# Merge of a two-layer mixer trunk: latent heads' products first, and a planner with twelve more, randomly shifted plans

## The chip, the cores and the metric

One core of one Trainium2 chip runs the whole program. The metric is device time in microseconds (us) of one execution; the kernel before was run three times for it, and once more under the profiler.

## The reference

Two layers over x of 512 positions by 1024 channels, float32. In each layer

```
h = rmsnorm(x); p = h @ w_in            # columns: three mixers, their gates, three merge gates
o_a = latent attention (8 heads, low-rank q and kv, rotary part) * silu(gate_a)
o_b = forgetting attention (8 heads, cumulative log forget gate) * silu(gate_b)
o_c = RWKV-7 time mixing (8 heads, delta-rule state) * silu(gate_c)
merged = sigmoid(g_a) * (o_a @ w_pa) + sigmoid(g_b) * (o_b @ w_pb) + sigmoid(g_c) * (o_c @ w_pc)
x = x + merged @ w_out
```

o_a, o_b and o_c have 512 channels each, the merge gates g_a, g_b, g_c 1024 each. What follows is about the order in which the three products of `merged` are made.

## The kernel before, in words

Activations lie transposed: channels on 128 partitions, the 512 positions along a row. A float32 matrix product is made of two rounded parts of each operand (`split`, line 679: a high part, and what is left of it), so one product over 128 input channels is three matmuls of 128x512 (`mm3`, lines 794 to 796). Weights come from DRAM by SP's queue (`wload`, line 758) and are split on ACT, DVE or POOL (`wpart`: the high part by `copy`, line 662, the low part by `combine`, line 674).

The body of a layer is written as five generators, run by `weave`: "p" prepares the four head pairs of RWKV, "c" runs their chains (`rwkv_chain`), "y" is the attention (four pairs of latent heads, then four pairs of forgetting heads, each softmax tile going PE, DVE, ACT, DVE, PE), "z" (`merge_gates`) projects the 24 merge gates and writes tanh of each to DRAM (`thd`), and "m" (`merge`) is the merge.

`merge` waits for the four chains and the four latent pairs. It makes tiles for the split o_a (`oa`, in the buffers "At" of the chains), o_c (`oc`, in "T3" and "KR") and o_b (`ob`), and loads o_a and o_c from DRAM (`odr`; `load`, line 1541) pair by pair, through tiles of the pool "tx", which has eight buffers. Then, for each of eight blocks d of 128 output channels, it loads the gates a and c (lines 1563 and 1564, into "tx"), makes the A product of the block (12 matmuls, PSUM tag "xk"), the C product (12 matmuls, tag "ch"), and on DVE (th + 1) * product for each (line 1556, which empties the PSUM buffer); A and C are added on POOL, and kept in `sums_` for d from 3 (tiles `sum` in buffers that RWKV has left) or written to `thd` for d of 0 to 2. The B products (tags "wk", "av", "xk", "ch") follow when the forgetting heads are closed, and last the products with w_out in tag "acc". PSUM buffers: "acc" 3, "wk" 2, "xk", "ch" and "av" 1 each.

What order the instructions take on each engine is set by `plan`. It lists the program's instructions with a cost each (`_cost`) and a table of latencies between engines, and runs a list scheduler over them (`forward`): on each engine the ready instruction with the greatest urgency goes next, and some may go to ACT, DVE or POOL. Tiles of a pool tag are granted in the order of the program, and the first uses of two tiles of one tag keep that order (`ops[uses[y][0]].after.setdefault(uses[x][0], False)`). One plan is made from urgencies by longest path, then ROUNDS = 3 more from urgencies that `backward` reads off the best plan so far. Each is replayed with latencies stretched by SLACK, and the shortest replay is kept. `kernel` does so for two margins and builds the program with the better one; each engine takes its instructions in exactly that order.

Of the kernel before, what the change touches and what calls it, by code (L numbers as in the profile page):

```python
# [83 lines left out]
WIRE, AHEAD = 250, 1500  # L84
ROUNDS = 3
PB = {"acc": 3, "wk": 2, "xk": 1, "ch": 1, "av": 1}
DRY = {"raw": 4, "w": 6, "acc": 1}
# [112 lines left out]
def port(op, e, psum):  # L200

    srcs = [a for a in op.ins if a[5] > 1 or a[2] - a[1] == 1]
    if e == POOL:
        return 2 if op.kind != "InstMemset" else 1
    if e != DVE or op.kind in ("InstMemset", "InstTensorReduce", "InstStreamTranspose", "InstReciprocal"):
        return 0
    n = op.outs[0][5]
    full = [a for a in op.ins if a[0] not in psum and a[5] >= n]
    if len(full) > 1:
        return 1  # L210
    return 2 if (op.kind in ("InstTensorCopy", "InstActivation", "InstTensorScalarPtr") and len([a for a in op.ins if a[5] >= n]) == 1
                 and full and op.outs[0][0] not in psum) else 0


def plan(insts, tags, manual, flex, margin, replay=None):
# [306 lines left out]
    best = None  # L522
    for i in range(1 + ROUNDS):
        if i:
            backward(best[1][2])
        last = forward()
        stretch[0] = SLACK
        real = forward(last[0])
        stretch[0] = margin
        if best is None or max(real[2]) < max(best[0][2]):  # L530
            best = real, last
# [18 lines left out]
def build(tc, x_t, wpk, wsm, wv, vec, cst, out, order_of=None, pick={}, queues=None, margin=2.0):  # L550
# [189 lines left out]
    for l in range(L):  # L740
# [415 lines left out]

        ready, built, done, closed, zdone = [], [0], [0], [0], [0]

# [353 lines left out]
        def merge_gates():  # L1512

            for d in range(8):
                for i in range(3):
                    th = T(tag="zth", bufs=1)
                    yield from proj(f"m{'abc'[i]}{d}", "z", lambda ps: act.activation(th, ps, AF.Tanh, scale=0.5))
                    nc.sync.dma_start(thd[d, i], th)
                zdone[0] += 1
# [11 lines left out]
        def merge():  # L1531
# [18 lines left out]
            def product(w, c, o, tag, th):  # L1550
                ps = PS(tag)
                for k in range(4):
                    mm3(ps, *w(c + 128 * k, c + 128 * k + 128), *o[k], k == 0, k == 3)
                    if k % 2:
                        yield
                dve.scalar_tensor_tensor(th, th, 1.0, ps, op0=ALU.add, op1=ALU.mult)

            sums_ = [None] * 3 + kept()
            for d in range(8):
                while zdone[0] <= d:  # L1560
                    yield "wait"
                ta, tc_ = TX(), TX()
                nc.sync.dma_start(ta, thd[d, 0])
                nc.sync.dma_start(tc_, thd[d, 2])
                yield from product(wgroup(f"pab{d}", "m"), 0, oa, "xk", ta)
                yield from product(wgroup(f"pc{d}", "m"), 0, oc, "ch", tc_)
                if sums_[d] is None:
                    combine(ta, ta, tc_, ALU.add, POOL)
                    nc.sync.dma_start(thd[d, 0], ta)
                else:  # L1570
                    combine(sums_[d], ta, tc_, ALU.add, POOL)
                yield
# [20 lines left out]

        steps, ob, mgk = [], [], []
        weave([("p", rwkv_preps()), ("c", rwkv_chains()), ("y", attention()), ("z", merge_gates()), ("m", merge())],
# [24 lines left out]
    if queues is None:  # L1620
        ops, queues, start, end, picked = plan(insts, tags, manual, flex, margin)
        raise Traced(max(end), stream_order(all_steps, ops, start), picked, queues)
    for q in queues:
# [147 lines left out]
```

## Time and profile before

| | us |
|---|---|
| median of 3 runs | 1400.03 (1399.03 to 1400.41) |
| the profiled execution | 1399.46 |
| its span, first to last instruction | 1397.7 |
| PE busy | 1333.1 (95%) |
| DVE busy | 1078.8 (77%) |
| ACT busy | 943.4 (67%) |
| POOL busy | 362.5 (26%) |
| mean granted PE clock | 0.985 of full speed |

PE's busy time counts a matmul until its modelled end, and matmuls overlap, so a stretch in which PE is busy throughout can still do more or less work; the count of matmuls in a stretch tells. An engine's idle time matters here only where PE waits for it.

### The profile page before, as it was taken

How to read it: one execution, taken by the hardware profiler on the slowest of the kernel's cores; microseconds unless marked ns; L12 is line 12 of the kernel's file. 1: busy time of each engine (PE TensorE's matmuls, PEld its weight loads, DVE VectorE, ACT ScalarE, POOL GpSimd, SP SyncE). 2: the span in 40 equal slices, each digit the busy share in tenths (PEclk: the TensorE clock that was granted, in tenths of full speed). 3: DMA queues.
4: the chain of work that ended last, by engine and by line, in shares of the span. 5: the costliest groups of instructions: out<-in, count | busy, mean ns of one | idle time of the engine just before them, and what ended most of it. 6: DMA issues, size and time to landing. Idle time of an engine off the chain costs nothing. (4 is left out here: it accounts for less than half of the span.)

```text
span 1397.7 us, 25030 instructions
## 1 busy us (share of the span) xinstructions
PE 1333.1 (95%) x8532; PEld 1051.7 (75%) x8532; DVE 1078.8 (77%) x2488; ACT 943.4 (67%) x1900; POOL 362.5 (26%) x749
## 2 busy tenths in 40 slices
PE   7999999999999999799999999999999999996998
PEld 5877787878778867578877787877777768874787
DVE  8967968877897687567688679788889697886673
ACT  7658676766987787524566777776878686875341
POOL 1343351215411611000021443531264125210000
PEclk9999999999999999799999999999999999998999
DMA  5443332334143231465534343322233333324763
GB/s 179 135 119 108 91 113 70 106 92 107 43 128 91 91 95 57 126 211 177 180 97 153 100 123 94 104 80 73 88 87 89 90 114 95 106 77 131 216 203 98
DMA packets 114623, 158.67 MB, mean 114 GB/s; under 512 B 36544, under 2 KB 44608, under 8 KB 114496
## 3 DMA queue, kind: packets, MB, share of 16 engines
q1 hardware_dynamic: 114496, 157.08, 37.3%
q8 instruction: 67, 1.10, 0.3%
q14 instruction: 60, 0.49, 0.1%
HBM read 128.72 MB, written 28.31 MB: 112 GB/s over the span
## 5 line engine op out<-in xcount | busy, mean ns | idle before, releaser
L794 PE MATMUL acc<-hh,w 128*128 128x512 f32 x1008 | 372.0, 404 | 18.3 <-DVE hh L662 5.4
L662 ACT ACTIVATE w<-raw 128x256 fp32r<-128x256 f32 (+1 forms) x521 | 208.2, 412 | 254.7 <-PE acc L796 145.3
L795 PE MATMUL acc<-hl,w 128*128 128x512 f32 x1008 | 369.2, 402 | 0.6 <-DVE hl L674 0.5
L796 PE MATMUL acc<-hh,w 128*128 128x512 f32 x1008 | 368.5, 401 | 1.0 <-DVE w L674 1.0
L674 DVE TENSOR_TENSOR w<-raw,w 128x256 fp32r<-128x256 f32 (+1 forms) x598 | 251.2, 434 | 81.4 <-ACT w L662 75.0
L794 PEld LDWEIGHTS acc<-hh,w 128*128 128x128 f32 x1008 | 189.1, 189 | 60.6 <-DVE hh L662 5.4
L796 PEld LDWEIGHTS acc<-hh,w 128*128 128x128 f32 x1008 | 189.3, 189 | 39.6 <-DVE w L674 2.5
L795 PEld LDWEIGHTS acc<-hl,w 128*128 128x128 f32 x1008 | 189.2, 189 | 39.4 <-DVE hl L674 1.9
L674 POOL TENSOR_TENSOR w<-raw,w 128x256 fp32r<-128x256 f32 (+1 forms) x102 | 92.8, 915 | 395.3 <-ACT w L662 199.7
L1019 POOL TENSOR_TENSOR W<-W,NL 128x60 f32<-128x60 f32 (+24 forms) x248 | 89.4, 361 | 75.1 <-DMA NL<-d 56.8
L1226 PE MATMUL wk<-qk 96*128 96x512 f32 (+11 forms) x320 | 93.7, 326 | 2.0 <-DVE PP L674 1.4
L662 DVE CAST w<-raw 128x256 fp32r<-128x256 f32 (+1 forms) x179 | 53.4, 306 | 48.3 <-PE acc L796 42.2
L1021 POOL TENSOR_TENSOR W<-W 128x60 f32<-128x60 f32 (+24 forms) x248 | 85.3, 344 | 18.2
L1226 PEld LDWEIGHTS wk<-qk 96*128 96x128 f32 (+2 forms) x320 | 59.8, 191 | 18.1 <-DVE PP L674 8.2
L674 DVE TENSOR_TENSOR PP<-wk,PP 128x512 fp32r<-128x512 f32 (+3 forms) x128 | 61.4, 486 | 14.7 <-ACT PP L662 13.2
L1201 DVE CUSTOM_DVE_ANT_0 wk<-wk,cmask 128x128 f32<-128x128 f32 (+3 forms) x128 | 61.7, 499 | 5.4 <-PE wk L1200 3.3
L662 ACT ACTIVATE PP<-wk 128x512 fp32r<-128x512 f32 (+3 forms) x120 | 50.9, 432 | 7.8 <-PE av L1240 3.6
L1227 DVE TENSOR_TENSOR wk<-wk,dmask 128x128 f32<-128x128 f32 x128 | 37.0, 293 | 14.8 <-PE wk L1226 13.8
L1238 PE MATMUL av<-PP,Vh 128*128 128x512 f32 (+3 forms) x128 | 43.6, 340 | 3.3 <-DVE PP L662 2.0
L1231 ACT ACTIVATE wk<-wk 128x512 f32<-128x512 f32 (+1 forms) x64 | 26.8, 423 | 28.7 <-DVE wk L1227 28.2
L1240 PE MATMUL av<-PP,Vh 128*128 128x512 f32 (+3 forms) x128 | 43.7, 342 | 1.3 <-DVE PP L674 1.3
L1200 PE MATMUL wk<-qk 96*128 96x384 f32 (+7 forms) x128 | 41.1, 334 | 2.2 <-DVE ty L1201 1.8
(536 smaller groups left out, 2885.0 us busy)
## 6 DMA issues: line engine op xcount, KB each, us to landing
raw<-wpk SPq DMA_DIRECT2D x326, 256.0 KB, 2.7
tx<-thd SPq DMA_DIRECT2D x54, 256.0 KB, 3.4
thd<-zth SPq DMA_DIRECT2D x48, 256.0 KB, 2.1
tx<-odr SPq DMA_DIRECT2D x22, 256.0 KB, 2.9
raw<-wpk SPq DMA_DIRECT2D x32, 128.0 KB, 2.2
NL<-d SPq DMA_DIRECT2D x32, 128.0 KB, 2.8
odr<-sg SPq DMA_DIRECT2D x14, 256.0 KB, 2.3
x<-x_t SPq DMA_DIRECT2D x8, 256.0 KB, 4.0
```

The lines of the kernel that those rows point to most:

```text
L662: lambda q: act.activation(dst, src, AF.Copy) if q == ACT else dve.tensor_copy(dst, src))
L674: any_of(costs, lambda q: (dve if q == DVE else gp).tensor_tensor(dst, a, b, op=op))
L794: pe.matmul(ps, wh, xh, start=first, stop=False)
L795: pe.matmul(ps, wh, xl, start=False, stop=False)
L796: pe.matmul(ps, wl, xh, start=False, stop=last)
L1019: gp.tensor_tensor(tv, WL[:, 0:m, s:s + 1].broadcast_to([128, m, n]), NL[:, s:s + 1, s + 1:32].broadcast_to([128, m, n]), op=ALU.mult)
L1021: gp.tensor_tensor(WL[:, 0:m, s + 1:32], WL[:, 0:m, s + 1:32], tv, op=ALU.add)
L1200: pe.matmul(ps[:, 0:n], t[sr, A["sq"], 128 * i:n], t[sr, 2, 0:n], start=True, stop=True)
L1201: dve.tensor_tensor_reduce(out=ps[:, 0:n], in0=ps[:, 0:n], in1=cmask[:, 512 - n:512], scale=1.0, scalar=NEG, op0=ALU.add, op1=ALU.max, acc ...
L1226: pe.matmul(pv, t[rows, k, js], t[rows, q, q0:512], start=i == 0, stop=i == len(passes) - 1)
L1238: pe.matmul(av[:, q0:512], vh, ph, start=j == 0, stop=False)
L1240: pe.matmul(av[:, q0:512], vh, pl, start=False, stop=j == 3)
```

## The change

In the merge the loop over the blocks is split in two. The first makes all eight A products, in the order d = 3, 4, 5, 6, 7, 0, 1, 2, and `merge_gates` projects the gates in that order; for d from 3 the gate is loaded straight into the kept tile `sum` and the product is made in place, for d of 0 to 2 a tile of "tx" is held (`tas`). The second makes the C products and adds. A and C both take PSUM tag "acc", counted by `open_` as the projections are.

In the planner twelve more plans (SEARCH) are made for each margin: each takes the urgencies from `backward` on the best plan, with a margin drawn between 1.2 and 2.0, and adds to every instruction a shift drawn between -2000 and 2000 ns, one for each tensor written. The best is now chosen by `score`: the end of the modelled plan plus half of WINDOW for every stretch of WINDOW ns (but for the first five and the last) in which PE's modelled work fills less than half.

```diff
+WINDOW = 3413
+SEARCH, JITTER = 12, 2000
...
+def score(ops, queues, start, end, *_):
+
+    work = defaultdict(float)
+    for a, b in zip(queues[PE], queues[PE][1:]):
+        s, e = start[a], min(start[b], start[a] + dict(ops[a].costs)[PE])
+        while s < e:
+            w = int(s // WINDOW)
+            work[w] += min(e, (w + 1) * WINDOW) - s
+            s = (w + 1) * WINDOW
+    last = int(start[queues[PE][-1]] // WINDOW)
+    return max(end) + WINDOW / 2 * sum(work[w] < WINDOW / 2 for w in range(5, last))
...
-    for i in range(1 + ROUNDS):
+    draw = random.Random(1)
+    for i in range(1 + ROUNDS + SEARCH):
         if i:
+            stretch[0] = margin if i <= ROUNDS else draw.uniform(1.2, 2.0)
             backward(best[1][2])
+            if i > ROUNDS:
+                shift = defaultdict(lambda: draw.uniform(-JITTER, JITTER))
+                for op in ops:
+                    op.urgency += shift[op.outs[0][0] if op.outs else op.kind]
...
-        if best is None or max(real[2]) < max(best[0][2]):
+        if best is None or score(ops, *real) < score(ops, *best[0]):
...
-            for d in range(8):
+            for d in (3, 4, 5, 6, 7, 0, 1, 2):
                 for i in range(3):
...
             def product(w, c, o, tag, th):
-                ps = PS(tag)
+                while tag == "acc" and not dry and open_[0] >= PB["acc"]:
+                    yield "wait"
+                open_[0] += tag == "acc"
+                ps = PS(tag, "m")
...
             sums_ = [None] * 3 + kept()
-            for d in range(8):
-                while zdone[0] <= d:
+            for i, d in enumerate((3, 4, 5, 6, 7, 0, 1, 2)):
+                while zdone[0] <= i:
                     yield "wait"
-                ta, tc_ = TX(), TX()
+                ta = sums_[d] if sums_[d] is not None else TX()
                 nc.sync.dma_start(ta, thd[d, 0])
+                yield from product(wgroup(f"pab{d}", "m"), 0, oa, "acc", ta)
+                if sums_[d] is None:
+                    tas[d] = ta
+            for d in (0, 1, 2, 3, 4, 5, 6, 7):
+                tc_ = TX()
                 nc.sync.dma_start(tc_, thd[d, 2])
-                yield from product(wgroup(f"pab{d}", "m"), 0, oa, "xk", ta)
-                yield from product(wgroup(f"pc{d}", "m"), 0, oc, "ch", tc_)
+                yield from product(wgroup(f"pc{d}", "m"), 0, oc, "acc", tc_)
                 if sums_[d] is None:
-                    combine(ta, ta, tc_, ALU.add, POOL)
-                    nc.sync.dma_start(thd[d, 0], ta)
+                    combine(tas[d], tas[d], tc_, ALU.add, POOL)
+                    nc.sync.dma_start(thd[d, 0], tas[d])
                 else:
-                    combine(sums_[d], ta, tc_, ALU.add, POOL)
+                    combine(sums_[d], sums_[d], tc_, ALU.add, POOL)
```

The plan is a new one from end to end. Line numbers of the layer's code are 22 higher in the change up to `load`, and up to 30 higher behind it. The buffers are named with their numbers below: mT3 and mKR (mT and mKR in the trace's rows) hold the high and low parts of o_c, mAt those of o_a, av and wk are attention's PSUM tiles, ch with bd the sums of a chain's normalization.

**PE, layer 1, where the first C product stands.** Before, right behind the last matmuls of attention:

```order
L1238 MATMUL av_6694<-PP_6735,Vh_1590 128x256
L1239 MATMUL av_6694<-PP_6735,Vl_1591 64x256
L1240 MATMUL av_6694<-PP_6735,Vh_1590 128x256
L1238 MATMUL av_6694<-PP_6746,Vh_1590 128x128
L1239 MATMUL av_6694<-PP_6746,Vl_1591 64x128
L1240 MATMUL av_6694<-PP_6746,Vh_1590 128x128
L794 MATMUL ch_6872<-mT3_6801,w_6875 128x512
L795 MATMUL ch_6872<-mKR_6802,w_6875 128x512
L796 MATMUL ch_6872<-mT3_6801,w_6875 128x512
```

In the change:

```order
L1260 MATMUL av_6705<-PP_6710,Vh_1634 128x512
L816 MATMUL acc_7017<-mAt_6747,w_7029 128x512
L1261 MATMUL av_6705<-PP_6710,Vl_1635 64x512
L817 MATMUL acc_7017<-mAt_6748,w_7029 128x512
L1262 MATMUL av_6705<-PP_6710,Vh_1634 128x512
L818 MATMUL acc_7017<-mAt_6747,w_7029 128x512
L816 MATMUL acc_7041<-mT3_6749,w_7044 128x512
L1248 MATMUL wk_6736<-qk0_4218 128x128
L817 MATMUL acc_7041<-mKR_6750,w_7044 128x512
L1248 MATMUL wk_6736<-qk0_4218 128x128
L818 MATMUL acc_7041<-mT3_6749,w_7044 128x512
```

The first C product stood behind the end of attention, with one A product made by then; now it stands behind all eight A products, with the last pair of forgetting heads still among the products around it.

**SP, layer 1, what is issued around the last pair of o_c.** odr<-KV writes it, the tx<-odr behind it reads it back, tx<-thd loads gates. Before:

```order
L1518 DMA thd_106<-zth_6384 128x512
L758 DMA raw_7023<-wpk 128x512
L743 DMA vc_7916<-vec 128x251
L1155 DMA odr_105<-KV_6165 128x512
L1541 DMA tx_6838<-odr_105 128x512
L1563 DMA tx_6846<-thd_106 128x512
L1564 DMA tx_6847<-thd_106 128x512
L1563 DMA tx_6896<-thd_106 128x512
L1564 DMA tx_6897<-thd_106 128x512
```

In the change:

```order
L1540 DMA thd_106<-zth_6399 128x512
L780 DMA raw_6994<-wpk 128x512
L780 DMA raw_7018<-wpk 128x512
L765 DMA vc_7911<-vec 128x251
L1177 DMA odr_105<-KV_6091 128x512
L1563 DMA tx_6786<-odr_105 128x512
L780 DMA raw_7042<-wpk 128x512
L1589 DMA tx_6967<-thd_106 128x512
L1589 DMA tx_6991<-thd_106 128x512
```

Before, the first gate load stands behind the read of o_c. In the change the five loads into the tiles sum stand higher, at rows 129 to 231 of SP's order (odr<-KV is row 244), and only the three gates a for d of 0 to 2 are left behind it.

**PE, layer 1, the two sums of the last chain's normalization.** Before:

```order
L1238 MATMUL av_6575<-PP_6651,Vh_1590 128x128
L1239 MATMUL av_6575<-PP_6651,Vl_1591 64x128
L1240 MATMUL av_6575<-PP_6651,Vh_1590 128x128
L690 MATMUL ch_6655<-PP_6656,bd_95 128x512
L691 MATMUL ch_6655<-PP_6656,bd_95 128x512
L690 MATMUL ch_6669<-PP_6670,bd_95 128x512
L1238 MATMUL av_6694<-PP_6699,Vh_1590 128x512
L691 MATMUL ch_6669<-PP_6670,bd_95 128x512
```

In the change:

```order
L818 MATMUL acc_6431<-hh_121,w_6498 128x512
L817 MATMUL acc_6400<-hl_122,w_6489 128x512
L712 MATMUL ch_6420<-PP_6421,bd_95 128x512
L816 MATMUL acc_6431<-hh_121,w_6498 128x512
L1260 MATMUL av_6543<-PP_6548,Vh_1634 128x512
L818 MATMUL acc_6400<-hh_121,w_6489 128x512
L713 MATMUL ch_6420<-PP_6421,bd_95 128x512
L1261 MATMUL av_6543<-PP_6548,Vl_1635 64x512
L1248 MATMUL wk_6563<-qk0_4218 128x256
L1262 MATMUL av_6543<-PP_6548,Vh_1634 128x512
L1248 MATMUL wk_6563<-qk0_4218 128x256
L817 MATMUL acc_6431<-hl_122,w_6498 128x512
L816 MATMUL acc_6795<-mAt_6747,w_6798 128x512
```

The sums (ch with bd) stood at the end of attention's rows; now they stand among gate projections, before the A products.

Counted over the whole order (columns are the widths of the matmuls' outputs added up):

| what stands where | before: matmuls, columns | change: matmuls, columns |
|---|---|---|
| layer 1, last chain's end to first C product | 98, 42,752 | 189, 85,504 |
| layer 1, second sum to first C product | 15, 4,096 | 157, 69,120 |
| layer 2, last chain's end to first C product | 42, 15,744 | 154, 68,096 |
| layer 2, second sum to first C product | 15, 4,096 | 125, 53,248 |
| layer 1, end of attention to its use in a B product | 194, 99,328 | 56, 28,672 |
| layer 2, end of attention to its use in a B product | 192, 98,304 | 51, 26,112 |
| columns ahead of the last chain's end, layer 1; layer 2 | 1,024,352; 2,366,336 | 1,015,648; 2,344,960 |
| mean between two of the chains' 48 state steps | 2,668 columns | 2,904 columns |
| low halves of weights on DVE, on POOL | 598, 102 | 569, 131 |

## Rows read from the trace of the kernel before

**Rows 1.** The page, parts 1 and 2: busy us per engine; granted clock, 40 slices.
```profile
PE 1333.1 (95%) x8532; PEld 1051.7 (75%) x8532; DVE 1078.8 (77%) x2488; ACT 943.4 (67%) x1900; POOL 362.5 (26%) x749
...
PEclk9999999999999999799999999999999999998999
```

**Rows 2.** PE timeline, layer 1 around the merge (start us, us, engine, line, operation).
```profile
548.68 0.87 PE L1128 MATMUL ch<-KR 64*64 64x64 f32 x24
...
564.29 0.39 PE L796 MATMUL xk<-mAt,w 128*128 128x512 f32 x1
...
570.89 0.63 PE L691 MATMUL ch<-PP,bd 128*128 128x512 f32 x1
...
577.52 0.47 PE L1240 MATMUL av<-PP,Vh 128*128 128x128 f32 x1 [1.06 <-DVE PP L674]
...
583.68 0.79 PE L794 MATMUL ch<-mT,w 128*128 128x512 f32 x1 [5.69 <-ACT mT L662]
```

**Rows 3.** SP timeline, the same stretch: DMA issues.
```profile
578.09 0.33 SPq L1155 DMA_DIRECT2D odr<-KV  x1
...
580.27 0.33 SPq L1541 DMA_DIRECT2D tx<-odr  x1
...
580.70 0.38 SPq L1563 DMA_DIRECT2D tx<-thd  x1
```

**Rows 4.** DVE timeline, the same stretch.
```profile
586.65 0.68 DVE L674 TENSOR_TENSOR sg<-do 128x512 f32<-128x512 f32 x1
...
587.25 0.68 DVE L1556 SCALAR_TENSOR_TENSOR tx<-tx,xk 128x512 f32<-128x512 f32 x1
```

**Rows 5.** PE timeline, layer 2 around the merge.
```profile
1263.46 0.40 PE L796 MATMUL xk<-mAt,w 128*128 128x512 f32 x1
...
1278.16 0.79 PE L794 MATMUL ch<-mT,w 128*128 128x512 f32 x1 [5.72 <-ACT mT L662]
```

**Rows 6.** Stretches: length; busy (count) PE, PEld, DVE, ACT, POOL; PEclk; DMA share; GB/s.
```profile
564.52:583.68 19.16, 8.87 (x32) 6.19 (x30) 10.77 (x25) 16.39 (x27) 1.05 (x2) 0.62 0.29 97
583.68:589.81 6.13, 6.11 (x14) 4.26 (x15) 4.58 (x7) 1.40 (x3) 1.43 (x1) 0.51 0.79 252
590.00:630.00 40.00, 40.00 (x164) 29.58 (x163) 24.84 (x52) 11.37 (x28) 0.00 (x0) 1.00 0.66 203
670.00:710.00 40.00, 40.00 (x174) 32.47 (x173) 26.85 (x58) 22.18 (x44) 0.20 (x2) 1.00 0.54 165
1263.46:1278.16 14.70, 4.91 (x20) 2.55 (x19) 8.42 (x18) 14.00 (x22) 0.00 (x0) 0.80 0.17 53
1278.16:1286.16 8.00, 6.85 (x15) 5.05 (x16) 4.79 (x10) 1.63 (x4) 0.00 (x0) 0.51 0.76 266
1290.00:1330.00 40.00, 40.00 (x165) 29.82 (x164) 25.74 (x54) 12.29 (x31) 0.00 (x0) 1.00 0.69 211
```

**Rows 7.** Stretches with rwkv chains and attention, columns as in Rows 6.
```profile
40.00:560.00 520.00, 507.54 (x3626) 404.31 (x3625) 413.96 (x996) 387.92 (x783) 165.82 (x352) 1.00 0.33 97
760.00:1260.00 500.00, 485.76 (x3523) 384.45 (x3521) 406.53 (x974) 370.25 (x745) 169.95 (x356) 1.00 0.32 95
```

**Rows 8.** The page, part 5: low halves of the weights, DVE and POOL.
```profile
L674 DVE TENSOR_TENSOR w<-raw,w 128x256 fp32r<-128x256 f32 (+1 forms) x598 | 251.2, 434 | 81.4 <-ACT w L662 75.0
...
L674 POOL TENSOR_TENSOR w<-raw,w 128x256 fp32r<-128x256 f32 (+1 forms) x102 | 92.8, 915 | 395.3 <-ACT w L662 199.7
```

**Rows 9.** DVE timeline, layer 1, beginning.
```profile
38.63 1.22 DVE L737 SCALAR_TENSOR_TENSOR tx<-x,ng,zth 128x512 f32<-128x512 f32 x1
...
41.60 1.40 DVE L737 SCALAR_TENSOR_TENSOR tx<-x,ng,zth 128x512 f32<-128x512 f32 x2
```

**Rows 10.** POOL timeline, the same stretch.
```profile
38.39 2.07 POOL L674 TENSOR_TENSOR w<-raw,w 128x256 fp32r<-128x256 f32 x2
```

**Rows 11.** PE timeline, two steps of the last chain, layer 2.
```profile
1251.33 0.41 PE L1117 MATMUL ch<-KR,KV 128*128 128x64 f32 x2
...
1252.45 0.33 PE L1117 MATMUL ch<-KR,KV 128*128 128x64 f32 x2
```

More of the change, by code (lines that the diff above doesn't have):

```diff
@@ L2 @@
 import math
+import random
 from collections import defaultdict, deque
@@ L1155, in rwkv_chain @@
             nc.sync.dma_start(odr[2, p], y)
-        ready, built, done, closed, zdone = [], [0], [0], [0], [0]
+        ready, built, done, closed, zdone, oc_last = [], [0], [0], [0], [0], []
         def rwkv_preps():
@@ L1556, in product @@
                 dve.scalar_tensor_tensor(th, th, 1.0, ps, op0=ALU.add, op1=ALU.mult)
+                open_[0] -= tag == "acc"
             sums_ = [None] * 3 + kept()
-            for d in range(8):
-                while zdone[0] <= d:
+            for i, d in enumerate((3, 4, 5, 6, 7, 0, 1, 2)):
+                while zdone[0] <= i:
                     yield "wait"
-                ta, tc_ = TX(), TX()
+                ta = sums_[d] if sums_[d] is not None else TX()
                 nc.sync.dma_start(ta, thd[d, 0])
+                yield from product(wgroup(f"pab{d}", "m"), 0, oa, "acc", ta)
[3 more added lines that the diff above has]
+                tc_ = TX()
                 nc.sync.dma_start(tc_, thd[d, 2])
-                yield from product(wgroup(f"pab{d}", "m"), 0, oa, "xk", ta)
-                yield from product(wgroup(f"pc{d}", "m"), 0, oc, "ch", tc_)
+                yield from product(wgroup(f"pc{d}", "m"), 0, oc, "acc", tc_)
                 if sums_[d] is None:
-                    combine(ta, ta, tc_, ALU.add, POOL)
-                    nc.sync.dma_start(thd[d, 0], ta)
+                    combine(tas[d], tas[d], tc_, ALU.add, POOL)
+                    nc.sync.dma_start(thd[d, 0], tas[d])
                 else:
-                    combine(sums_[d], ta, tc_, ALU.add, POOL)
+                    combine(sums_[d], sums_[d], tc_, ALU.add, POOL)
                 yield
@@ L1592, in merge @@
                 yield
-        steps, ob, mgk = [], [], []
+        steps, ob, mgk, tas = [], [], [], {}
         weave([("p", rwkv_preps()), ("c", rwkv_chains()), ("y", attention()), ("z", merge_gates()), ("m", merge())],
@@ L1621, in build @@
         ops, queues, start, end, picked = plan(insts, tags, manual, flex, margin)
-        raise Traced(max(end), stream_order(all_steps, ops, start), picked, queues)
+        raise Traced(score(ops, queues, start, end), stream_order(all_steps, ops, start), picked, queues)
     for q in queues:
```

## The prediction

> **What bounds the kernel now.** I read the page first: PE is busy for 1333.1 of 1397.7 us, every other engine far less, and its granted clock falls below 9 tenths in only two of forty slices [rows 1]. So the kernel is bound by PE, and the question is where PE stands still or runs slowly. The two slices tell where to look: the seventeenth (559 to 594 us) and the thirty-seventh, the same place in layer 2. I then went through PE's timeline there, and looked up on SP and DVE who was late.
>
> In layer 1 the last chain's output leaves PE at 549.5 us, the first A product is done at 564.5, attention ends at 577.5, and then PE idles for 5.69 us, until the first C product at 583.68, which waits for ACT's high part of o_c [rows 2]. The reader should see in SP's rows why nothing fills that time: o_c's last pair is written at 578.09, read back at 580.27, and the gate for the first A product is loaded only behind that, at 580.70 [rows 3], though it had long been in DRAM. Loads into "tx" keep the order of the program. So the only PSUM buffer "xk" is held by the finished A product until DVE empties it at 587.25 [rows 4], 22.7 us after its last matmul, and seven more A products, whose operands are there, can't start. Layer 2 repeats it: last A matmul at 1263.46, first C matmul at 1278.16 [rows 5].
>
> **Term 1: the stall in layer 1.** At full clock with nothing missing PE did 174 matmuls of 128x512 in 40 us, 0.230 us each or 0.449 ns a column in the stretch from 670 to 710 [rows 6]. From 564.52 to 583.68 it did 32, mostly narrow ones of attention; their widths add up to 9,600 columns, so 4.3 us of work in 19.16 us: 14.9 us lost. From 583.68 to 589.81 the granted clock was 0.51, the lower of the two levels (1.2 GHz), after PE had been mostly idle; 13 products of 0.230 us, 3.0 us of work, took 6.13: 3.1 us lost. Together **18.0 us**.
>
> **Term 2: the stall in layer 2.** From 1263.46 to 1278.16 the widths add up to 6,144 columns, 2.8 us of work in 14.70 us: 11.9 lost. From 1278.16 to 1286.16 it is 15 products, 3.45 us of work, in 8.00 us at a clock of 0.51: 4.55 lost [rows 6]. Together **16.5 us**.
>
> **Does the change fill them?** The order says so. Between the chain's end and the first C product there are now 85,504 and 68,096 columns, which at 0.449 ns are 38.4 and 30.6 us of work. The need is no more than the old path: 549.5 to 583.68, 34.1 us in layer 1 [rows 2], of which much was the normalization's sums standing behind attention. Those sums now stand early: from the second of them to the first C product there are 69,120 and 53,248 columns, 31.0 and 23.9 us, while before the whole rest of the path (norm, gate, write, read, split) fitted between that sum's matmul at 570.89 and 583.68, 12.8 us [rows 2]. So o_c should be there 10 us or more before PE comes to it. The A products' gates for d from 3 go to tiles outside "tx", so they no longer queue behind the read of o_c; that is five products, 60 matmuls, 13.8 us. Only the last three gates still stand behind it on SP, and their products have three "acc" buffers to be finished in. I count both terms as gone: **-34.5 us**.
>
> **Term 3: one buffer each against three.** With one "xk" and one "ch", the products of 590 to 630 came at 164 in 40 us, and 165 in layer 2, against 174 on "acc" [rows 6]; PE counts as busy throughout, but 164 x (40/164 - 40/174) is 2.3 us lost, and 2.1 us in layer 2. Both products now use "acc". **-4.4 us**; the bounds are 0 (the projections still competing for "acc") and -4.4.
>
> **Term 4: what is late next.** The cover is taken from somewhere: attention now ends only 56 and 51 matmuls (28,672 and 26,112 columns, 12.9 and 11.7 us) ahead of the B products that need its last pair, where it had over 190. Before, the way from PE's last attention matmul, which ended at 578.0 [rows 2], to the gated output on DVE, done at 587.33 [rows 4], took 9.3 us, and with its split, two instructions of about 0.7 us as that one, about 11. That is nearly all of the cover, so I put a remaining wait of 1 us a layer: **+2 us**. Bounds: 0, and 8.7 us a layer if the bare tail of before came back (first rival).
>
> **Term 5: the rest of the plan.** All other instructions are reordered too. In the two long stretches of chains and attention PE idled 12.5 and 14.2 us, 26.7 us of 1020 [rows 7]. Twelve further plans can find better places or worse ones: the chosen one is best by a model, and its waits here are short ones all over, which the model need not place well. The chains' 48 state steps keep their filler (2,904 columns between two steps, against 2,668). I take 0, with half of the idle time either way as bounds: -13 to +13 us. DVE gives 29 low halves of weights to POOL, which takes 0.915 us for one where DVE takes 0.434 [rows 8]: 29 x 0.481 = 14 us of longer work on an engine that was idle 74% of the span [rows 1]. Cost 0, covered by the weights being split ahead of their use; without that cover, the 14 us.
>
> **Where a rule speaks against it.** In the trace the same DVE instruction took 1.22 us beside two POOL subtractions of weights, and 0.70 us each when POOL stood still [rows 9, 10], so 29 more of them on POOL can cost DVE 29 x 0.52 = 15 us, little more than the 29 x 0.434 = 12.6 us that it is relieved of [rows 8]. The net, 2.5 us on an engine with 23% to spare, is nothing on PE's path. The Trainium skill (SBUF — State Buffer, "Who interferes with whom") goes further: the port pair that VectorE and GpSimd share is an exclusive lock, so the later one stands still for the whole of the other's instruction. The row shows 0.52 us, not the whole of a POOL instruction of 1.03 us. By the rule the price would be 29 x 1.03 = 30 us of DVE time, an estimate, and with all of it on PE's path 1393 us.
>
> **Sum.** 1399.46 (the profiled execution) - 34.5 - 4.4 + 2 = 1362.6. The median of the runs shown lies 0.6 above the profiled execution, so I predict **1363 us**, 2.6% less.
>
> **The rivals.**
>
> *The stall only moves to the end of attention* (chance 0.14). PE takes its rows in order; if the last pair's output is late for the B products, PE stands there and the clock falls as it did at 583.68. Price: the bare tail of about 1.3 heads cost 13.0 us for some 4.3 us of work before, 8.7 us a layer. For it: cover of 12 us against a path of 11. Against it: DVE has no o_c to split then. Time: 1363 - 2 + 2 x 9 = 1379.
>
> *POOL's extra work reaches PE* (0.05). If each of the 29 low halves stood on the path for its longer time, 14 us: 1377. Against it: POOL stood idle 395 us ahead of its 102, half of it waiting for ACT's high halves [rows 8], so it is not short of time.
>
> *The search is worth more* (0.05). Over half of the idle time in the long stretches goes, and some at the layers' seam: below 1350, say 1345.
>
> *The merge isn't relieved* (0.03). o_a or its gates come as late as o_c in spite of the order, because the A products wait for buffers of the last chain. Then terms 1 to 3 stay: 1398 to 1402, no change. Against it: before, the first A product ran 15 us after the chain's end and well ahead of o_c.
>
> *Slower: the last chains run bare* (0.03). To win time at the merge, the last chain ends after 3.9 us (layer 1) and 9.6 us (layer 2) less of PE's work than before. Its steps are a loop between PE and DVE: two steps started 1.12 us apart [rows 11]; with no filler PE would be idle for about 0.9 of that. There are 48 state steps and as many other dependent ones in the eight chains. The point from which it decides: 39 us / 0.9 = 43 of the 96 steps bare. With 60 bare the time is 1363 + 54 = 1417. Against it: the order shows 2,000 columns or more, 0.9 us, in nearly every state step, as before.
>
> **How the numbers follow.** My forecast, 1350 to 1376 (term 5's bounds), has 0.70. About 0.2% (3 us) is what a measurement of this kernel can tell from no change. Faster by more: 0.70 + 0.14 + 0.05 + 0.05 = 0.94; within it 0.03; slower 0.03. The range has to reach the first rival to hold 8 in 10: from 1350 to 1384 (1379 and part of term 5's spread above it), which holds also the second and leaves out 1345, 1400 and 1417.
>
> **What would show it.** Right, if the first C product shows no idle time before it, the granted clock stays 1.00 around both merges, matmuls of A and C come at some 174 in 40 us, DVE empties each A product within a microsecond or two, and the idle time of PE outside the merges is still 20 to 35 us. Term 4 is wrong if PE waits longer than 2 us before a B product; term 5, if PE's idle time in the long stretches leaves 13 to 40 us. The whole is wrong if PE still waits for o_c, or if A products wait for the parts of o_a or for their gates.

## The result, and the profile after

The change takes **1365.44 us** (median of 4 runs, 1364.29 to 1366.35), the kernel before 1399.53 beside it (1398.60 to 1400.41): a ratio of **0.9756**, 95% interval 0.9739 to 0.9773, so 34.1 us or 2.4% faster. 1363 was predicted.

The page of the change, parts 1 and 2 (busy us by engine, then the granted clock in tenths, 40 slices), answers to [rows 1]:

```profile
PE 1318.9 (97%) x8532; PEld 1049.0 (77%) x8532; DVE 1070.8 (78%) x2430; ACT 934.5 (68%) x1905; POOL 407.5 (30%) x794
...
PEclk9999999999999999999999999999999989999999
```

The two slices with a low clock, in the middle of the merges, are gone. One other is there now, at some 1110 us, in the chains of layer 2. PE's timeline where the first C product starts, layer 1 and then layer 2 (start us, us, engine, line, operation; idle time before it in brackets), answers to [rows 2, 5]:

```profile
582.52 0.39 PE L818 MATMUL acc<-mAt,w 128*128 128x512 f32 x1
582.75 0.40 PE L816 MATMUL acc<-mT,w 128*128 128x512 f32 x1
...
608.56 0.40 PE L816 MATMUL wk<-mKB,w 128*128 128x512 f32 x1
...
1264.76 0.40 PE L816 MATMUL acc<-mAt,w 128*128 128x512 f32 x1
1265.00 0.40 PE L816 MATMUL acc<-mT,w 128*128 128x512 f32 x1
```

No bracket stands at 582.75 or 1265.00, where 5.69 and 5.72 us of idle time stood, and none at 608.56, where the first B product starts. SP and POOL in layer 1 show why:

```profile
558.35 0.33 SPq L1177 DMA_DIRECT2D odr<-KV  x1
560.36 0.33 SPq L1563 DMA_DIRECT2D tx<-odr  x1
...
562.45 1.38 SPq L1589 DMA_DIRECT2D tx<-thd  x3
...
571.58 1.29 POOL L696 TENSOR_TENSOR mKR<-tx,mT 128x512 fp32r<-128x512 f32 x1
```

The last pair of o_c is written at 558.35, against 578.09 [rows 3], and the last split of o_c is done at 572.87, 9.9 us ahead of the C products (in layer 2 at 1260.39, 4.6 us ahead). Stretches of the change (length; busy time and count of PE; granted clock; DMA share; GB/s), for [rows 6, 7]:

```profile
40.00:560.00 520.00, 511.81 (x3640) 1.00 0.34 103
560.00:590.00 30.00, 27.78 (x126) 1.00 0.48 150
600.00:640.00 40.00, 40.00 (x173) 1.00 0.64 203
760.00:1250.00 490.00, 473.74 (x3434) 0.99 0.34 98
1290.00:1330.00 40.00, 40.00 (x173) 1.00 0.67 218
```

**An account of the time.** For every kernel I added up PE's idle time as its timeline records it, and what the granted clock is short of 1.00 while PE was busy. Idle time at the lower clock counts as idle alone, or it would be counted twice. The rest of the span is work at full clock, gaps that are not recorded, and the span's two ends. The last column is another cut, by equal work: in every kernel the widths of all matmuls add up to 2,713,920 columns, so the times that two kernels need from one number of columns to another can be compared. It has the two merges together, from 1,061,792 to 1,258,656 columns and from 2,437,184 to 2,618,176: from the end of the last chain in the change to the last B matmul in the kernel before. (These are counted in the trace; the table of the change has the columns ahead of the chain's end lower, by 46,144 and 92,224 for both kernels, which leaves their differences as they are.)

| | time | ratio, 95% | span | idle | clock | rest | merges |
|---|---|---|---|---|---|---|---|
| before | 1399.53 | | 1397.7 | 57.9 | 12.9 | 1326.9 | 214.2 |
| the change | 1365.44 | 0.9739 to 0.9773 | 1364.6 | 39.7 | 4.9 | 1320.0 | 183.8 |
| e1, merge alone | 1369.50 | 0.9765 to 0.9795 | 1368.4 | 40.8 | 8.3 | 1319.3 | 192.5 |
| e2, planner alone | 1390.91 | 0.9918 to 0.9947 | 1389.3 | 48.4 | 16.7 | 1324.2 | 201.0 |
| e3, plans chosen by end | 1379.24 | 0.9839 to 0.9869 | 1376.4 | 44.9 | 9.6 | 1321.9 | 180.2 |
| e4, one buffer each | 1379.85 | 0.9848 to 0.9881 | 1377.8 | 47.7 | 6.4 | 1323.7 | 198.9 |
| e5, order from 0 | 1370.76 | 0.9778 to 0.9807 | 1368.0 | 40.9 | 4.7 | 1322.4 | 177.8 |
| e6, start 5 | 1380.03 | 0.9841 to 0.9874 | 1379.0 | 46.6 | 7.3 | 1325.1 | 181.2 |
| e7, start 18 | 1364.88 | 0.9737 to 0.9767 | 1363.3 | 39.4 | 1.7 | 1322.2 | 182.8 |
| e8, charge alone | 1371.21 | 0.9785 to 0.9814 | 1372.0 | 42.7 | 7.7 | 1321.6 | 194.3 |
| e9, e8 with one step moved | 1372.50 | 0.9796 to 0.9825 | 1372.9 | 41.9 | 9.5 | 1321.5 | 194.1 |
| e10, start 8 | 1361.83 | 0.9716 to 0.9745 | 1359.8 | 38.1 | 8.1 | 1313.6 | 181.9 |
| e11, start 80 | 1361.72 | 0.9704 to 0.9737 | 1360.3 | 36.0 | 8.3 | 1316.0 | 179.4 |

From before to the change the span falls by 33.1 us: idle time by 18.2, clock by 8.0, the rest by 6.9. By equal work 30.4 of it lie in the two merges (14.5 in layer 1, 15.9 in layer 2): 16.3 idle, 9.6 clock, 4.5 rest. The expectations of e6, e10 and e11 reckon with an earlier rest, near 1319, in which idle time at the lower clock was taken off twice.

### The profile page after: what moved, and what is told of

The parts are those of the page before. It is cut to its first block, busy times and chain, and to the rows that moved or that the text cites. A ratio compares the mean times of both kernels' runs of the same rounds, so it can differ in the third digit from the quotient of the medians.

```text
span 1364.6 us, 25008 instructions
## 1 busy us (share of the span) xinstructions
PE 1318.9 (97%) x8532; PEld 1049.0 (77%) x8532; DVE 1070.8 (78%) x2430; ACT 934.5 (68%) x1905; POOL 407.5 (30%) x794
## 4 chain that ended last, share of the span: by engine, by line
PE 71%; DVE 15%; ACT 11%; issue 3%; DMA 0%; SPq 0%; DVEq 0%; ACTq 0%
PE acc L817 16%; PE acc L816 16%; PE acc L818 16%; PE wk L1248 3%; PE ch L1099 2%; DVE w L696 2%; ACT w L684 1%; PE av L1260 1%; PE av L1262 1%; DVE qk L684 1%; PE wk L816 1%; PE av L1261 1%; DVE PP L696 1%; PE xk L1018 1%; PE wk L818 1%
## 5 line engine op out<-in xcount | busy, mean ns | idle before, releaser
L684 ACT ACTIVATE w<-raw 128x256 fp32r<-128x256 f32 (+1 forms) x544 | 216.6, 412 | 199.1 <-PE acc L818 162.7
L696 DVE TENSOR_TENSOR w<-raw,w 128x256 fp32r<-128x256 f32 x569 | 245.5, 444 | 73.4 <-ACT w L684 69.1
L696 POOL TENSOR_TENSOR w<-raw,w 128x256 fp32r<-128x256 f32 (+1 forms) x131 | 116.4, 895 | 399.5 <-ACT w L684 251.8
L1043 POOL TENSOR_TENSOR W<-W 128x60 f32<-128x60 f32 (+24 forms) x248 | 94.2, 380 | 18.1
L1248 PE MATMUL wk<-qk 96*128 96x512 f32 (+9 forms) x320 | 95.8, 319 | 3.5 <-DVE PP L696 2.4
L1248 PEld LDWEIGHTS wk<-qk 128*128 128x128 f32 (+2 forms) x320 | 59.9, 189 | 17.5 <-DVE PP L696 6.6
L684 DVE CAST w<-raw 128x256 fp32r<-128x256 f32 (+1 forms) x156 | 46.9, 307 | 31.2 <-PE acc L818 26.0
L1253 ACT ACTIVATE wk<-wk,ncum 128x512 f32<-128x512 f32 (+1 forms) x64 | 31.3, 494 | 21.6 <-DVE wk L1249 21.4
L817 PE MATMUL acc<-mKR,w 128*128 128x512 f32 x128 | 46.0, 397 | 0.0
L684 ACT ACTIVATE KV<-ch 64x256 f32<-64x256 f32 (+2 forms) x65 | 32.7, 503 | 18.0 <-PE ch L1150 10.7
```

Of the source, the lines that this page charges most:

```text
L684: lambda q: act.activation(dst, src, AF.Copy) if q == ACT else dve.tensor_copy(dst, src))
L696: any_of(costs, lambda q: (dve if q == DVE else gp).tensor_tensor(dst, a, b, op=op))
L817: pe.matmul(ps, wh, xl, start=False, stop=False)
L1043: gp.tensor_tensor(WL[:, 0:m, s + 1:32], WL[:, 0:m, s + 1:32], tv, op=ALU.add)
L1248: pe.matmul(pv, t[rows, k, js], t[rows, q, q0:512], start=i == 0, stop=i == len(passes) - 1)
L1253: act.activation(pv, pv, AF.Exp, scale=A["scale"], bias=b)
```

## The experiments

Each is an edit of the change, and each but e9 has a plan of its own from end to end. The theory: the reordered merge carries the gain, and the new planner little. The rival: the search and its charge carry a good part.

**e1, the merge alone.**

```diff
-SEARCH, JITTER = 12, 2000
+SEARCH, JITTER = 0, 2000
...
-        if best is None or score(ops, *real) < score(ops, *best[0]):
+        if best is None or max(real[2]) < max(best[0][2]):
```

> The new merge with the old planner: one plan from the unshifted urgencies beside the old ones, chosen by its end alone. Theory (the reordered latent heads carry the gain, the search and the idle charge nothing of their own): 1365 us, 1358 to 1373, ratio 0.970 to 0.981; PE without idle before the first C product, both merges at a clock of 1.00. Rival (the search and the charge carry a third or more): 1378 us or more, ratio over 0.985.

1369.50 us, 30.3 less than the kernel before beside it (1399.82): nearly all of the gain comes with the old planner. The size is as the theory has it; two signs aren't: in layer 2 PE waited 2.54 us before the first C product, and the clock was 0.83 from 1270 to 1280. By equal work its merges take 8.7 us more than the change's, and all else 4.8 less.

**e2, the planner alone.** The parts of `merge_gates` and `merge` in the diff are undone.

```diff
-            for i, d in enumerate((3, 4, 5, 6, 7, 0, 1, 2)):
+            for d in range(8):
...
-                yield from product(wgroup(f"pab{d}", "m"), 0, oa, "acc", ta)
+                yield from product(wgroup(f"pab{d}", "m"), 0, oa, "xk", ta)
+                yield from product(wgroup(f"pc{d}", "m"), 0, oc, "ch", tc_)
```

> The old merge with the new planner: twelve more plans, choice by end and PE's charged idle. Theory: the dependency that stalls PE (the products on o_c behind its round trip through memory) is still there, so 1390 to 1402 us, ratio 0.993 to 1.002, with pauses of some 6 us each left in the middle of the merges. Rival (a search with a charge for idle steps fills the pauses with other work): 1380 us or less, ratio under 0.986, pauses under 2 us.

1390.91 us, 8.9 us less than the kernel before beside it (1399.82). PE's timeline of e2 in layer 2, around the first C product:

```profile
1264.13 0.39 PE L818 MATMUL xk<-mAt,w 128*128 128x512 f32 x1
1272.32 0.80 PE L816 MATMUL ch<-mT,w 128*128 128x512 f32 x1 [7.81 <-ACT mT L684]
```

and ACT's split ahead of it:

```profile
1271.64 1.15 ACT L684 ACTIVATE mT<-tx 128x512 fp32r<-128x512 f32 x2 [5.62 <-DMA odr<-KV]
```

In layer 2 the pause is there, and longer; in layer 1 there was none ahead of the C product, and attention stood still instead (3.37 and 2.04 us, at 564.02 and 569.45). So a better choice of plan can move such a pause, and twelve more plans did not remove both. By equal work its merges take 13.2 us less than before, where the change's take 30.4 less, and all else 4.8 more.

**e3, the plans chosen by their end.** As e1's second edit, with SEARCH left at 12.

> The new merge with all twelve more plans, but the plan is chosen by its end alone, without the charge for PE's idle stretches. Theory: within 8 us of the change, 1357 to 1373 us, ratio 0.970 to 0.981: no pause is left that the charge would have to see. Rival (the charge picks a plan that is clearly better on the chip): 1375 us or more, ratio over 0.982.

1379.24 us, 13.8 more than the change and 9.7 more than e1. The theory missed, though not in the merges: by equal work they take 180.2 us, 3.6 less than in the change, and all else 15.4 more. PE's timeline of e3 shows one of two places, then the stretches around both (columns as above):

```profile
330.40 0.39 PE L818 MATMUL acc<-hh,w 128*128 128x512 f32 x1
334.19 0.79 PE L816 MATMUL acc<-hh,w 128*128 128x512 f32 x1 [3.41 <-ACT ty L1450]
```

```profile
60.00:70.00 10.00, 4.24 (x16) 0.69 0.08 18
70.00:80.00 10.00, 10.00 (x57) 0.80 0.41 117
330.00:340.00 10.00, 6.59 (x18) 0.67 0.24 79
```

Around pauses of 2.94 (at 65) and 3.41 us the clock was at its lower level (1.2 GHz) for some microseconds: it was short by 3.1 + 2.0 us at the first, 1.9 of them while PE was idle anyhow, and by 3.3 at the second, 0.4 of them idle. Such pauses are what the charge counts. That a plan without the two was taken with the charge, and one with them without it, is one pair of plans; e8 against e1 is another, and there the charge gained nothing.

**e4, one buffer each.** A goes back to "xk", C to "ch".

```diff
-                yield from product(wgroup(f"pab{d}", "m"), 0, oa, "acc", ta)
+                yield from product(wgroup(f"pab{d}", "m"), 0, oa, "xk", ta)
...
-                yield from product(wgroup(f"pc{d}", "m"), 0, oc, "acc", tc_)
+                yield from product(wgroup(f"pc{d}", "m"), 0, oc, "ch", tc_)
```

> The change, but the products of A leave through the one xk buffer and those of C through the one ch buffer, as before, in place of the three acc buffers; the plan that comes out may differ elsewhere. Theory (the tile's release sets some 164 in place of 174 matmuls in 40 us, 2.2 us a layer): 1367 to 1374 us, ratio 0.976 to 0.982, with 164 to 168 matmuls in 40 us in the stretch of the C products. Rival (buffers do not matter, the rate went up for another reason): 1363 to 1367 us with 172 or more. Second rival (a release that is late starves PE wholly): over 1380 us.

1379.85 us, more than the theory gave. PE's waits in e4 (engine, line, waited for: us in total, times, longest):

```profile
PE xk L816 <- DVE sum L1581: 3.9, 4, 1.6
PE ch L816 <- DVE tx L1581: 2.6, 4, 1.1
```

In the change the same waits, for L1581 to empty a tile, come to 0.8 us in all, so 5.7 us are the buffers', shown as idle time. But the waits are only part of it. By equal work the whole difference lies in the merges, 198.9 us against 183.8: 7.5 of it idle, 1.5 clock, and 6.1 in which PE was busy but slower; all else takes 1.9 less. So one buffer each costs this order some 15 us, with one plan to judge by. That is more than term 3's size. A likely reason, not tried by itself, is the order: before, A and C products took turns in two buffers, while here all eight A products follow each other through one. From 600 to 640 there were 174 matmuls, narrow ones among them, so the rate of that stretch says nothing on the 164 to 168 expected.

**e5, the order from 0.** Both loops over A and its gates run d = 0 to 7.

```diff
-            for i, d in enumerate((3, 4, 5, 6, 7, 0, 1, 2)):
+            for i, d in enumerate((0, 1, 2, 3, 4, 5, 6, 7)):
```

> The change, but the latent and kv products go through the output blocks 0 to 7 in order, in place of 3 to 7 and then 0 to 2, so that the three blocks whose sums have to wait in tx tiles come first. Theory (the three tx tiles are held for the whole of the latent products and the round trip of o_c shares tx and SP with them, so it lands later): 1368 to 1380 us, with a pause of 1 us or more ahead of the first C product in at least one layer. Rival (o_c has about 10 us to spare, so the order costs nothing that is not the plan's own scatter): 1358 to 1373 us and no pause ahead of the first C product.

1370.76 us and no pause ahead of either first C product: the rival's signs. The time alone lies in both ranges, and inside the scatter of e6 and e7. The order of the blocks isn't what relieves the merge. Nor is it that the first gates no longer queue behind the read of o_c: here, as before, they stand right behind it on SP (554.55 behind 554.18, in layer 1), and with three buffers it costs nothing, for o_c is written at 552.0, before the first A product begins at 557.3.

**e6 and e7, other starts of the random numbers.** `random.Random(1)` becomes `random.Random(5)` and `random.Random(18)`.

> The change with another start of the random numbers (5 for 1), nothing else: a different plan of the same work. By the planner's own reckoning the plan is 10.8 us later than that of the change, charges included (1358.2 for 1347.4; of the 43 starts tried it is among the poorer). Theory (time is a fixed 1318 to 1320 us of work at full rate, plus PE's recorded idle time, plus what its clock falls short; plans differ in the last two): 1368 to 1380 us, and the span less idle and clock loss within 2 us of 1319. Rival (the starts do not matter on the chip): 1362 to 1368 us.

> The change with the start 18 for the random numbers: by the planner's own reckoning the best of 43 starts, 9.3 us before the change and with no charged stretch at all (1338.1 for 1347.4). Theory (the charge sees the pauses that cost time on the chip): 1350 to 1362 us, faster than the change, with under 40 us of recorded idle and under 7 us of clock loss. Rival (the planner's reckoning is too coarse at this size): 1362 to 1378 us.

1380.03 and 1364.88 us. In e6 the merges are clean (181.2 us by equal work) and the time went elsewhere, 17.0 us more than in the change: 1.69 and 2.72 us of idle time at 133.54 and 137.53, with the clock at 0.81 and 0.68 in the two stretches there (130 to 140, 140 to 150), and a rest 5.1 us above the change's, so the rest is not fixed as I had assumed. In e7 the best plan by the planner's reckoning, a model's figure and no time, was no faster on the chip than the change; there the rival was right.

**e8, the charge alone.** SEARCH is 0, the choice by `score` stays.

> The new merge, no further plans, but the choice among the four plans of a pass by end and charge. Theory (the new merge gives the bulk, the charge some microseconds by which plan it takes): 1362 to 1375 us; by the planner's reckoning it lies between the change and the merge with neither (1362.8, against 1347.4 and 1367.0). Rival (the charge misleads when there is little to choose from): 1376 us or more.

1371.21 us, inside the theory's range, but with the pause back, and no better than e1 (1369.50), the same code without the charge: with four plans to choose from the charge gained nothing. SP, DVE and PE of e8 in layer 1:

```profile
586.47 0.33 SPq L1177 DMA_DIRECT2D odr<-KV  x1
588.74 0.33 SPq L1563 DMA_DIRECT2D tx<-odr  x1
...
591.98 2.49 DVE L696 TENSOR_TENSOR mKR<-tx,mT 128x512 fp32r<-128x512 f32 x4
594.39 1.87 DVE L1581 SCALAR_TENSOR_TENSOR tx<-tx,acc 128x512 f32<-128x512 f32 x3
```

```profile
589.82 0.40 PE L818 MATMUL acc<-mAt,w 128*128 128x512 f32 x1
595.21 0.76 PE L816 MATMUL acc<-mT,w 128*128 128x512 f32 x1 [4.99 <-DVE tx L1581]
```

In this plan the sums of the last chain's normalization stand late again: the first at 573.11, 14.0 us behind the chain's end at 559.08, where in the change it stands 1.9 us behind (540.14, 538.25). So the A products are nearly used up when o_c is written, 3.8 us before the last of them ends, and the pause is 4.99 us. DVE's row adds a link that the prediction did not have: the three finished A products fill all three acc buffers, and DVE empties them only behind four splits of o_c.

**e9, the first emptying ahead of the splits.** The plan of e8, with one DVE instruction in each layer moved up.

```diff
+    old = list(q)
+    for i in range(1, len(q)):
+        j = i if empties(old[i]) and not empties(old[i - 1]) else 0
+        while j and low(q[j - 1]):
+            q[j - 1], q[j] = q[j], q[j - 1]
+            j -= 1
```

> The kernel of the charge alone, with its plan kept as it is but for one DVE instruction in each layer: the first emptying of a finished A product, which stood behind four (layer 1) or one (layer 2) of the splits of o_c, goes ahead of them, so that the first C product finds a free acc buffer sooner. Theory (of the 4.99 us that PE paused there in layer 1, the part up to the landing of o_c and its first split, some 2.5 us, is the round trip; the rest is DVE's order, which fills all three acc buffers): first pause 2 to 3 us, with up to 1 us more behind it for the low half of o_c; time 1366 to 1371 us. Rival (the pause is the round trip of o_c alone): pause 4.5 to 5.5 us, time within 2 us of 1371.2.

PE's timeline of e9, and DVE's, in layer 1:

```profile
592.44 0.47 PE L816 MATMUL acc<-mT,w 128*128 128x512 f32 x1 [2.88 <-DVE tx L1581]
593.28 0.50 PE L817 MATMUL acc<-mKR,w 128*128 128x512 f32 x1 [0.38 <-DVE mKR L696]
...
595.69 0.80 PE L816 MATMUL acc<-mT,w 128*128 128x512 f32 x1 [1.67 <-DVE tx L1581]
```

```profile
591.60 0.69 DVE L1581 SCALAR_TENSOR_TENSOR tx<-tx,acc 128x512 f32<-128x512 f32 x1 [0.54 <-DMA tx<-thd]
592.21 0.42 DVE L684 CAST mT<-tx 128x512 fp32r<-128x512 f32 x1
592.54 2.49 DVE L696 TENSOR_TENSOR mKR<-tx,mT 128x512 fp32r<-128x512 f32 x4
594.95 1.28 DVE L1581 SCALAR_TENSOR_TENSOR tx<-tx,acc 128x512 f32<-128x512 f32 x2
```

The first pause fell from 4.99 to 2.88 us, as expected, so the order on DVE did set its end; now a gate does, for which DVE's emptying waits 0.54 us, loaded behind the read of o_c. But 0.38 and 1.67 us follow, because the next buffers are emptied behind the splits all the same: 4.93 in place of 4.99, and the time is 1372.50, above the 1366 to 1371 expected and no less than e8's 1371.21. The wait only moved. What would help is o_c written earlier, which no run tried with this plan.

**e10 and e11, two more starts.** `random.Random(8)` and `random.Random(80)`.

> The change with the start 8 for the random numbers: by the planner's own reckoning 1343.0, 4.4 us before the change and 4.9 behind the start 18. Theory (the chip's time follows the planner's only to some 6 us, so no gain of this size can be planned): 1360 to 1372 us, with the remainder after idle and clock loss at 1317 to 1323. Rival (the better reckoning shows on the chip): under 1360 us.

> The change with the start 80: by the planner's own reckoning 1343.3, 4.1 us before the change. Theory: 1360 to 1372 us, as for the start 8, the remainder at 1317 to 1323. Rival: under 1360 us, which would beat every kernel so far.

1361.83 and 1361.72 us, as the theory said; the rival's gain did not show. By the two intervals e11 lies under the change (0.9704 to 0.9737 against 0.9739 to 0.9773), by 3.7 us; e10's overlaps it. Both rests, 1313.6 and 1316.0, lie below the 1317 expected, and over the thirteen kernels the rest ranges over 13 us, so idle time and clock do not account for the difference of two plans to better than that.

## Why the prediction was right, term by term

- **Terms 1 and 2, the stalls: -34.5 predicted, -25.9 measured.** In the two merges, by equal work, idle time fell from 21.8 to 5.5 us and the clock's loss from 9.6 to nothing. The terms were too large in two places. They priced the narrow matmuls of attention inside the stalls at 0.449 ns a column, 4.3 and 2.8 us; with idle time and clock taken out, these took 5.7 and 5.0, so of the 34.5 only 30.7 was lost time. And they counted the stalls as wholly gone, where 5.5 us of short waits are left, most of them attention's (0.27 to 1.35 us each).
- **What the pause hung on was read too simply.** The prediction has the first C product wait for o_c's round trip. The split that it waited for stood on ACT behind attention's last division (tile do: a logarithm and an exponential of the softmax sums, each with a table load of 1.28 us). Layer 1 before, then layer 2:

```profile
581.18 1.28 ACT L1255 ACT_TABLE_LOAD   x1
582.48 0.63 ACT L1255 ACTIVATE do<-do 128x512 f32<-128x512 f32 x1
583.01 1.65 ACT L662 ACTIVATE mT<-tx 128x512 fp32r<-128x512 f32 x3
...
1276.96 0.63 ACT L1255 ACTIVATE do<-do 128x512 f32<-128x512 f32 x1
1277.50 1.14 ACT L662 ACTIVATE mT<-tx 128x512 fp32r<-128x512 f32 x2
1278.87 0.63 ACT L662 ACTIVATE mT<-tx 128x512 fp32r<-128x512 f32 x1 [0.24 <-DMA tx<-odr]
```

  In layer 1 the read of the last pair had landed just then, at 582.86, so division and round trip ended together; in layer 2 ACT waits for the read only after the first C product has begun (1278.16). In e2, with no division in the way, it was the store of the last pair for which ACT's split waited (5.62 us). The change covers both, so the forecast did not suffer.
- **That the merge carries most of the gain is shown.** e1 has the old planner and keeps 30 of the 34 us; e2 has the new planner without the new merge, keeps a pause of 7.81 us and gains 9. All ten kernels with the new merge and three buffers took 1361.7 to 1380.0 us, e2 1390.9.
- **Term 3, three buffers: -4.4 predicted, and it held.** DVE and PE before, where a C product hands over to the next in the one buffer ch:

```profile
596.37 0.69 DVE L1556 SCALAR_TENSOR_TENSOR tx<-tx,ch 128x512 f32<-128x512 f32 x1 [1.15 <-PE ch L796]
...
596.87 0.40 PE L794 MATMUL xk<-mAt,w 128*128 128x512 f32 x1
...
597.20 0.47 PE L794 MATMUL ch<-mT,w 128*128 128x512 f32 x1
...
597.51 0.39 PE L795 MATMUL xk<-mAt,w 128*128 128x512 f32 x1
```

  The next product starts right behind DVE's emptying (597.06), and 0.33 and 0.31 us lie between starts that are 0.23 apart elsewhere; such gaps are too short to be recorded as idle. Such places add up to 2.2 us from 590 to 630 and 2.0 from 1290 to 1330; the change has none in its two stretches, which go at 173 matmuls in 40 us. e2, with the single buffers and another plan, has 165 again (1280 to 1320). The rest of the merges' time fell by 4.5 us. That figure alone would not show it, for in the ten kernels with three buffers it ranges over 4.6.
- **Term 4, a wait behind attention: +2 predicted, nothing there.** The B products start with no idle time before them. The cover of 11.7 to 12.9 us was enough, and the first rival did not come.
- **Term 5, the rest of the plan: 0 with bounds of 13 either way; -2.7 measured.** Outside the merges idle time went from 36.0 to 34.2 us (20 to 35 were named as the sign), the clock's loss from 3.3 to 4.9. By equal work layer 1 took 6.7 us less ahead of its merge, and layer 2 4.0 more. In the two long stretches of chains and attention PE idled 24.5 us (13 to 40 were named), so the chains did not run bare. How wide it can go is shown by five starts of the same code, four of them picked by the planner's reckoning from its better and its poorer end: 1361.7, 1361.8, 1364.9, 1365.4 and 1380.0 us.
- **Luck.** Terms 1 and 2 were 8.6 us too large, terms 4 and 5 came out 4.7 lower than put, and the errors offset each other in part. And no term knows which plan is drawn: 1363 came within 2.4 us of this one, and within 17 of start 5.
- **The signs and rivals.** The sign that DVE empties each A product within a microsecond or two can be read only for the first (1.8 us behind its last matmul), since the others' matmuls mix; PE waited 0.8 us in all for an emptying. "The merge isn't relieved" had 0.03 and did not happen in the change, but e8 shows it is closer than that: same code, pauses of 4.99 and 2.83 us. The order alone isn't what counts, but how long before the end of the A products o_c is written. Over ten kernels with the new merge and three buffers, 20 merges: with 13 us or more (24.6 and 18.5 in the change) no wait ahead of the first C product; with 11.2, 8.2, 7.5, 6.9 and 3.8 us waits of 0.5, 1.1, 2.5, 2.8 (2.2 in e9) and 5.0 us (2.9 and 1.7 in e9). The prediction compared the path with the plan's columns and was right on that, without asking what fixes them.
- "The search is worth more" would have read below 1350; e1 against the change puts the whole planner at 4 us with this merge, less than the starts differ. "POOL's extra work reaches PE" is not seen: no wait of PE in the change is put down to POOL, though it took 131 low halves, and DVE's own took 444 ns each for 434 [rows 8]:

```profile
L696 DVE TENSOR_TENSOR w<-raw,w 128x256 fp32r<-128x256 f32 x569 | 245.5, 444 | 73.4 <-ACT w L684 69.1
...
L696 POOL TENSOR_TENSOR w<-raw,w 128x256 fp32r<-128x256 f32 (+1 forms) x131 | 116.4, 895 | 399.5 <-ACT w L684 251.8
```

  The prediction misread rows 9 and 10 here: POOL's first subtraction began ahead of DVE's instruction, at 38.39, and ended at 39.31, and DVE ended 0.55 us later, at 39.86, so it did stand until POOL was done. The change shows the same in layer 2:

```profile
1258.40 1.44 POOL L696 TENSOR_TENSOR mKR<-tx,mT 128x512 fp32r<-128x512 f32 x1 [0.30 <-ACT mT L684]
...
1259.25 1.15 DVE L696 TENSOR_TENSOR mKR<-tx,mT 128x512 fp32r<-128x512 f32 x1
```

  DVE ends 0.55 us behind POOL again; such a subtraction takes it 0.69 us without POOL. With the rule of the Trainium skill (SBUF — State Buffer, "Who interferes with whom"), that the shared port pair is an exclusive lock, the trace agrees. The 30 us worked out from it, and 1393, did not come, because not every low half on POOL meets DVE, and one that does costs DVE only the rest of it: over 0.418 us each, the time without POOL, DVE's low halves of 128x256 lost 9.7 us before and 15.2 in the change, 5.4 more.

## What to carry to other kernels

Before a product that waits for a round trip through memory, put products whose operands are there, and then measure the slack: the store has to come at least the whole way (here 9 to 10 us from store to first use, splits and emptied buffers included) before that work ends; at 11.2 us there was still a wait of 0.5. Price a stall as idle time plus what the clock gives up while the engine is busy, here 21.8 and 9.6 us; counting the clock over the idle time as well would have made the 9.6 into 17.1. Where a planner makes the order, one change of code is one draw from a spread of plans (18 us over five starts), so a gain of a few microseconds is shown only against several plans, and the version to keep is picked by runs on the chip: e11 came out below the change, e7 and e10 beside it.

## What the runs showed of the hardware that was not expected

The same pause did not always cost the clock. At the seam of the layers the change waits 2.38 us at 701.22 and its clock stays at 1.00 in the stretches after it; e10 waits 2.43 us in the same place, and its clock is 0.51 from 700 to 704. Stretches of the change, then of e10:

```profile
700.00:704.00 4.00, 2.71 (x11) 1.00 0.14 53
704.00:708.00 4.00, 3.75 (x17) 1.00 0.08 5
```

```profile
696.00:700.00 4.00, 1.57 (x8) 1.00 0.42 129
700.00:704.00 4.00, 3.18 (x8) 0.51 0.01 2
704.00:708.00 4.00, 4.00 (x13) 0.64 0.20 73
```

In both PE had been busy throughout ahead of the pause. And no single long pause is needed: in the change the clock was 0.80 and then 0.50 around three waits of 0.37, 0.60 and 0.92 us at 1108.13, 1109.38 and 1110.81; it fell within the third:

```profile
1108.00:1112.00 4.00, 2.35 (x9) 0.80 0.24 64
1112.00:1116.00 4.00, 4.00 (x16) 0.50 0.64 154
```

So a kernel's loss to the clock can differ by some 3 us at one place behind nearly the same wait (in e10 a second wait, of 0.82 us at 701.77, came when the clock had fallen already, at 700.1), which is part of the scatter between plans. What decides it was not tried.
